# Later operand splits in two up products, S5 tables and convolution weight splits on VectorE, and a skip term folded into Toeplitz blocks

## The chip, the cores and the metric

The kernel runs on one core of one Trainium2 chip. The metric is the device time of one execution in microseconds, taken as the median of repeated runs. Five engines work side by side on a core: TensorE (PE, matrix products), VectorE (DVE), ScalarE (ACT), GpSimd (POOL) and SyncE (SP), which here issues nearly all transfers. Each executes its own instructions in the order in which they stand in its queue.

## What is computed

One layer of a diffusion backbone on 1,024 latent tokens and 256 context tokens, width 1,024, in float32:

```python
x   = half_step_ffn(x,   mods[0:3],   ffn1...)          # SwiGLU, 1024 -> 2*2816 -> 1024
ctx = half_step_ffn(ctx, mods_c[0:3], ffn1...)
# ctx passes the S5 scan once, to give the initial states h0s
p = modulate(rms_norm(x, mix_g_pre), ...) @ w_in;  bg, cg, v, u = split(p)
y_conv = bg * grid_short_conv(cg * v, conv_w)           # 512 channels
y = einsum(h_fwd, c).real + einsum(h_bwd, c).real + d_skip * u    # S5, 32 groups of 16
y = gelu(y);  y_ssm = y * sigmoid(y @ w_glu + b_glu)
x = x + mods[5] * rms_norm(concat(y_conv, y_ssm) @ w_out, mix_g_post)
x = half_step_ffn(x, mods[6:9], ffn2...)
```

`half_step_ffn` is `x + 0.5*gate*rms_norm((silu(g)*u) @ w_down)` with `g, u = split(modulate(rms_norm(x)) @ w_gu)`.

## The kernel before

**Arithmetic.** A float32 product is made of three passes: each operand is split into a high part (an ACT copy rounded to fp32r) and a low part (a DVE subtraction, operand minus high part), and PE adds high*high, high*low and low*high (`split`, L157; `hop` does it for an activation block, `wop` for a weight block, `wcols` for 128 columns of a weight). The latent up products (`g_lat`) and down products (`d_lat`) use a seven-product scheme: the tokens are two halves, the contraction is two halves, and products numbered 1 to 7 take blocks b11, b21, b12, b22 or their differences.

**Start of an up product.** `hops` (L562) goes through the stages 1, 2, 5, 3, 7, 6, 4, with four blocks (k = 0 to 3) in each. In stages 1, 2, 5 and 3 PE transposes the normalised tokens into PSUM and ACT evacuates a block with scale and shift; stages 5, 7, 6 and 4 subtract blocks in place on DVE. Each stage then splits its four blocks (`hop`: one ACT copy and one DVE subtraction of 128x512 each), one step behind. While this runs, PE does sixteen early products: for the first four column blocks f = 0 to 3 of the weight the products 1, 2, 5, 3, straight in float32 without splits. The first split products are (0,6), (1,6), (0,7), (1,7), (0,4), (1,4), then the same of f = 2, 3; the blocks of stage 2 and of stage 3 are first needed split by (4,2) and (4,3). The interleaving of `hops` steps (h), products (p, P), weight preparations (w) and norm steps is written out by hand in the strings `S1` (first up product) and `S2` (second).

**Order.** The order on each engine is fixed at build time by a scheduler that walks along a simulated timeline and takes the earliest ready instruction of the program. In the start of the first up product DVE and PE are held to program order (`G0`); in the second they are not.

**Context stage.** `g_ctx` makes the context's up product in 22 blocks f of 48 matmuls of 256 columns; a block's two weights are split one block ahead by `wcols`. Beside it runs `s5_prep`, which makes the S5 tables: four groups o of eight scan groups, each with six 128x1024 multiplications, additions or subtractions (`cmul`, in `s5_prep`, L1395), then transposes and small matmuls on PE. For o = 0 and 2 the six run on DVE, for o = 1 and 3 on POOL. At its end it builds the Toeplitz blocks of the short lags; lag zero is the tile `lag0`.

**Convolution and S5 stage.** `conv` (L1644) makes twelve products of 128 columns of `w_in` (48 matmuls each), whose weights `wcols` splits one weight ahead; the pattern `PC` puts six of the subtractions on POOL and the others on DVE. Its steps cover sixteen `s5_pair` steps: PE, then DVE (four short reductions, eight operations of 128x256 and two scans), then POOL (two multiplications of 128x512), DVE again, and PE, which waits for the result. After each four pairs `s5_out` (L1619) brings the result back through DRAM, loads `u` again (512 KB), adds the skip term `u*d` on DVE (128x1024) and applies the GELU. The string of numbers `UNITS` says how many convolution steps follow each pair.

Of the kernel before, what the change touches and what calls it, by code (L numbers as in the profile page):

```python
# [13 lines left out]
OP = mybir.AluOpType  # L14
AX = mybir.AxisListType

P = 128
# [7 lines left out]
G = 32  # L25
PAIRS = G // 2
H = 16
# [41 lines left out]
class Kernel:  # L69
# [492 lines left out]
    def hops(self, stages, blocks, hb, hr):  # L562

        t = [[], []]
        for src, m in stages:
            if src:
                x, f = src
                mm, one = blocks[x]  # L570
                if not t[x]:
                    t[x] = [self.z([P, 2, 512]) for _ in range(4)]
                pts = [mm(k + 4 * f) for k in range(4)]
                yield
            pend = None
            for k in range(4):
                if src:
                    one(k + 4 * f, t[x][k][:, f], pts[k])
                b11, b21 = (t[0][k][:, q] for q in range(2))
                b12, b22 = (t[1][k][:, q] if t[1] else None for q in range(2))  # L580
                if m == 5:
                    self.sub(b11, b12, b11)
                elif m == 7:
                    self.sub(b12, b22, b12)
                elif m == 6:
                    self.sub(b11, b22, b11)
                elif m == 4:
                    self.sub(b21, b21, b11)
                c = {1: b11, 2: b21, 3: b22, 4: b21, 5: b11, 6: b11, 7: b12}[m]
                if m in hr:  # L590
                    hr[m].append(c)
                if pend is not None:
                    hb[m].append(self.hop(pend))
                pend = c
                if k < 3:
                    yield
            hb[m].append(self.hop(pend))
            yield

    def postnorm_g(self, ys, gate, xsrcs, dsts):  # L600
# [794 lines left out]
    def s5_prep(self):  # L1395
        nc, i = self.nc, self.i
        pl = nc.gpsimd
        slot = lambda shape: self.t(self.zp, shape, "z")
        crs = [slot([P, 4, 2, 64]) for _ in range(2)]
        for k, nme in enumerate(("ssm_c_re", "ssm_c_im")):  # L1400
            for d in range(2):
                self.load(crs[k][:, :, d, :], i[nme][0, d].rearrange("(b g) h p -> (g h) b p", b=4))
        pw, br_ = slot([P, 2, 2, T8, 32]), slot([P, 2, 32, H])
        self.load(pw.rearrange("p w r t a -> p (w r t a)"), self.pwd)
        self.load(br_.rearrange("p r a h -> p (r a h)"), self.brd)
        yield
        czp = [slot([P, 32, 2, H]) for _ in range(2)]
        ct = slot([P, 2, 32, H])
        for k in range(2):
            pl.memset(czp[k], 0.0)  # L1410
        for _ in range(4):
            yield
        for k in range(2):
            pt = self.ps()
            for b in range(4):
                self.tr(pt[:, b * P : (b + 1) * P], crs[k][:, b].rearrange("p d n -> p (d n)"), P)
            self.ts(ct[:, k].rearrange("p a h -> p (a h)"), pt, 1.0 - 2 * k)
            for d in range(2):
                r = slice(64 * d, 64 * d + 64)
                nc.scalar.activation(czp[k][r, :, d, :], ct[r, k], AF.Copy)  # L1420
            yield
        kt_ = slot([P, G, 32])
        pdv = self.pd.rearrange("a p w -> p a w")
        shp = [P, 8, T8, H]

        def power(w, r, gs):
            return pw[:, w, r, :, gs].rearrange("p t a -> p a t").unsqueeze(3).to_broadcast(shp)

        for o in range(4):
            gs = slice(8 * o, 8 * o + 8)  # L1430
            xr, xi, xt = slot(shp), slot(shp), slot(shp)
            b0 = br_[:, 0, gs, :].unsqueeze(2).to_broadcast(shp)
            b1 = br_[:, 1, gs, :].unsqueeze(2).to_broadcast(shp)
            self.cmul(xr, xi, power(0, 0, gs), power(0, 1, gs), b0, b1, xt, pl if o % 2 else None)
            yield
            pk = self.ps()
            for a in range(8):
                for r, xx in ((0, xr), (1, xi)):
                    nc.tensor.matmul(
                        pk[:, 32 * a : 32 * a + 32],  # L1440
                        xx[:, a].rearrange("p t h -> p (t h)"),
                        czp[r][:, 8 * o + a].rearrange("p q h -> p (q h)"),
                        start=r == 0,
                        stop=r == 1,
                    )
            nc.vector.tensor_copy(kt_[:, gs, :], pk[:, :256].rearrange("p (a n) -> p a n", n=32))
            yield
            for r, xx in ((0, xr), (1, xi)):
                ev = slot([P, 8, P])
                for b in range(2):  # L1450
                    pt = self.ps()
                    for a in range(4):
                        self.tr(
                            pt[:, a * P : (a + 1) * P],
                            xx[:, 4 * b + a].rearrange("p t h -> p (t h)"),
                            P,
                        )
                    nc.scalar.activation(
                        ev[:, 4 * b : 4 * b + 4, :], pt.rearrange("p (a n) -> p a n", n=P), AF.Copy
                    )  # L1460
                c0 = BO + 256 * r
                self.load(
                    pdv[:, 4 * o : 4 * o + 4, c0 : c0 + 256], ev.rearrange("p (a q) n -> p a (q n)", q=2)
                )
                yield

        lag0 = slot([H, G, H])
        self.load(lag0, kt_[112:128, :, 0:H])
        self.add(lag0, lag0, kt_[0:16, :, H:])
        for t in range(T8):  # L1470
            r = slice(t * H, t * H + H)
            if t < 7:
                self.load(self.gd[:, :, 14 - t], kt_[r, :, 0:H])
            if t > 0:
                self.load(self.gd[:, :, 7 - t], kt_[r, :, H:])
        self.load(self.gd[:, :, 7], lag0)
        yield
        for t in range(T8):
            r = slice(t * H, t * H + H)
            self.load(self.td[r], self.gd[:, :, 7 - t : 15 - t].rearrange("h g l k -> h g (l k)"))  # L1480
            if t % TY == TY - 1:
                yield
        self.load(self.ctd, ct.rearrange("p r a h -> p (r a h)"))
# [135 lines left out]
    def s5_out(self, j, yps, dst=None):  # L1619
        nc = self.nc  # L1620
        ye = self.z([P, 4, 2, CL])
        for q in range(2):
            nc.scalar.activation(ye[:, :, q, :], yps[q].rearrange("p (a c) -> p a c", c=CL), AF.Copy)
        ydf = self.yd.rearrange("t h g c -> (t h) g c")
        self.load(ydf[:, 8 * j : 8 * j + 8, :], ye.rearrange("p a q c -> p (a q) c"))
        y = self.ta() if dst is None else dst
        yv = y.rearrange("p (t c) -> p t c", t=T8)
        for g in range(8):
            self.load(yv[H * g : H * g + H], self.yd[:, :, 8 * j + g, :].rearrange("t h c -> h t c"))
        u = self.ta()  # L1630
        self.load(u, self.ud[j * P : (j + 1) * P].rearrange("p t c -> p (t c)"))
        yield
        self.stt(y, u, self.ssmd(j), y, OP.mult, OP.add)
        nc.scalar.activation(u, y, AF.Square, scale=math.sqrt(0.044715))
        self.stt(u, u, 1.0, y, OP.add, OP.mult)
        nc.scalar.activation(u, u, AF.Tanh, scale=math.sqrt(2.0 / PI))
        self.stt(y, u, 1.0, y, OP.add, OP.mult)
        self.td_(u)
        if dst is None:
            self.load(self.zd[j], y)  # L1640
            self.td_(y)
        yield

    def conv(self, hi, lo, yc):  # L1644
# [5 lines left out]
        for p, c0 in enumerate(seq):  # L1650
# [5 lines left out]
            for h in range(2):  # L1656
# [3 lines left out]
                if h == 0 and p + 1 < len(seq):  # L1660
                    nxt = self.wcols(win, seq[p + 1], nc.gpsimd if PC[p % len(PC)] else None)
                if n == 0:
# [464 lines left out]


PP = PH = PU = 0
PC = (0, 1, 0, 0, 1, 0, 1, 1, 0, 1, 1, 1)  # L2130
FIVE = 4
SW = 520
QE = 0
# [70 lines left out]
```

## Time and profile before

| | us |
|---|---|
| median of 3 runs | 2041.51 |
| the three runs | 2045.14, 2041.51, 2039.92 |
| the profiled execution, its own time | 2045.32 |
| its span, first to last instruction | 2043.5 |
| PE busy in the span | 1949.4 (95%) |
| DVE busy | 1419.7 (69%) |
| ACT busy | 830.8 (41%) |
| POOL busy | 111.5 (5%) |
| mean granted TensorE clock | 0.985 of full speed |

The span and 1.8 us around it make the profiled time, which is 3.8 us above the median. PE is busy in all but 94 us of the span, so what a change can win lies in these 94 us, and in stretches where the clock granted to PE was below full speed. A row of the timeline tells when a run of equal instructions on an engine started, how long it took, how many there were (x), and in brackets how long the engine stood idle before it and what ended that.

### The profile page before, as it was taken

What the parts mean: (1) busy time and instruction counts of PE and PEld (TensorE: products, weight loads), DVE (VectorE), ACT (ScalarE), POOL (GpSimd) and SP (SyncE); (2) the same over time, 40 slices, a digit from 0 to 9 for tenths busy, and PEclk for the clock granted to TensorE, in tenths of its full rate; (3) what the DMA queues carried; (4) which work ended last, traced back from release to release, by engine and by line L of the source; (5) the groups of instructions that cost most, each with busy time, mean ns of one, the idle gap of its engine ahead of it and who ended that gap; (6) DMA issues with size and microseconds to landing.
All of it is one profiled execution on the core that took longest, in us unless ns stands there. A gap on an engine that the chain in (4) does not pass through costs nothing.

```text
span 2043.5 us, 25754 instructions
## 1 busy us (share of the span) xinstructions
PE 1949.4 (95%) x9364; PEld 1554.5 (76%) x9364; DVE 1419.7 (69%) x2548; ACT 830.8 (41%) x1463; POOL 111.5 (5%) x70
## 2 busy tenths in 40 slices
PE   7899999999899999999998899998999999999997
PEld 3477778888898978778787778764888888887775
DVE  1774459897753669797759885488855555577977
ACT  5432333434343445575432333364333333334543
POOL 0000000000420000000004430010000000000000
PEclk9999999999999999999999999998999999999999
DMA  9157642555679875566785433331632222277554
GB/s 331 31 191 255 249 141 83 144 158 162 196 222 257 284 262 176 199 234 232 215 279 165 165 113 114 103 124 56 206 110 73 93 88 78 88 269 271 185 183 162
DMA packets 328251, 354.94 MB, mean 174 GB/s; under 512 B 46976, under 2 KB 242236, under 8 KB 328124
## 3 DMA queue, kind: packets, MB, share of 16 engines
q1 hardware_dynamic: 325820, 344.91, 51.8%
q10 hardware_dynamic: 2304, 8.39, 1.0%
q8 instruction: 73, 1.20, 0.2%
q14 instruction: 54, 0.44, 0.1%
HBM read 280.61 MB, written 74.69 MB: 174 GB/s over the span
## 4 chain that ended last, share of the span: by engine, by line
PE 74%; DVE 15%; DMA 5%; issue 2%; ACT 2%; SPq 1%; POOL 1%; DVEq 0%; ACTq 0%; POOLq 0%
PE ps L51 74%; DVE z L51 6%; DVE t L51 5%; DVE w L51 3%; DMA wr<-in_ffn_w_down 1%; SPq L51 1%; DMA wr<-in_ffn_w_gu 1%; ACT t L51 1%; DMA z<-in_w_ada 1%; ACT w L51 1%; ACT z L51 1%; DMA z<-in_x 0%; POOL t L51 0%; DVE sy L51 0%; DMA wr<-t2d 0%
## 5 line engine op out<-in xcount | busy, mean ns | idle before, releaser
L51 PE MATMUL ps<-z,w 128*128 128x512 f32 (+1 forms) x5328 | 1144.4, 375 | 21.2 <-DVE w L51 6.9
L51 PEld LDWEIGHTS ps<-z,w 128*128 128x128 f32 x5328 | 931.2, 191 | 216.3 <-DVE w L51 7.9
L51 PE MATMUL ps<-w,w 128*128 128x512 f32 x1848 | 426.8, 392 | 15.4 <-DVE w L51 10.7
L51 PEld LDWEIGHTS ps<-w,w 128*128 128x128 f32 x1848 | 346.6, 188 | 93.8 <-DVE w L51 15.1
L51 ACT ACTIVATE w<-wr 128x512 fp32r<-128x512 f32 (+1 forms) x270 | 206.8, 767 | 360.3 <-PE ps L51 302.8
L51 DVE TENSOR_TENSOR w<-wr,w 128x512 fp32r<-128x512 f32 (+1 forms) x264 | 234.3, 889 | 117.5 <-ACT w L51 114.8
L51 ACT ACTIVATE w<-t 128x512 fp32r<-128x512 f32 x292 | 177.5, 626 | 183.0 <-DVE t L51 88.1
L51 DVE TENSOR_TENSOR w<-t,w 128x512 fp32r<-128x512 f32 x292 | 197.4, 687 | 75.1 <-ACT w L51 74.8
L51 DVE TENSOR_TENSOR t<-t,ps 128x512 f32<-128x512 f32 x150 | 102.5, 685 | 109.0 <-PE ps L51 108.3
L51 PE MATMUL ps<-z,t 128*128 128x512 f32 x512 | 147.1, 448 | 9.9 <-DVE t L51 8.8
L51 PEld LDWEIGHTS ps<-z,t 128*128 128x128 f32 x512 | 96.8, 190 | 58.3 <-issue 37.5
L51 ACT ACTIVATE t<-ps 128x512 f32<-128x512 f32 (+2 forms) x143 | 77.4, 542 | 147.8 <-PE ps L51 146.3
L51 ACT ACTIVATE w<-z 128x512 fp32r<-128x512 f32 x110 | 69.5, 632 | 144.7 <-PE ps L51 142.6
L51 DVE TENSOR_TENSOR z<-z,z 128x512 fp32r<-128x512 f32 (+3 forms) x139 | 114.3, 856 | 16.7 <-ACT z L51 11.7
L51 DVE TENSOR_TENSOR t<-wr 128x512 f32<-128x512 f32 x124 | 83.6, 686 | 20.3 <-DMA wr<-in_ffn_w_down 13.4
L51 ACT ACTIVATE t<-z 128x1024 bf16<-128x1024 f32 (+3 forms) x132 | 75.5, 605 | 48.4 <-DVE z L51 31.6
L51 DVE TENSOR_TENSOR w<-z,w 128x512 fp32r<-128x512 f32 x110 | 75.6, 687 | 24.2 <-ACT w L51 24.0
L51 ACT ACTIVATE t<-t 128x512 f32<-128x512 f32 (+1 forms) x83 | 51.8, 624 | 74.0 <-DVE t L51 73.3
L51 DVE TENSOR_TENSOR z<-t,ps 128x512 f32<-128x512 f32 (+1 forms) x52 | 29.8, 573 | 64.4 <-PE ps L51 64.4
L51 ACT ACTIVATE z<-z 128x512 fp32r<-128x512 f32 (+2 forms) x76 | 48.0, 678 | 56.0 <-DVE z L51 42.2
L51 PE MATMUL ps<-w,t 128*128 128x512 f32 x264 | 64.4, 401 | 1.9 <-DVE w L51 1.3
L51 ACT ACTIVATE z<-ps 128x512 f32<-128x512 f32 x74 | 41.6, 595 | 56.6 <-PE ps L51 56.5
(120 smaller groups left out, 1333.7 us busy)
## 6 DMA issues: line engine op xcount, KB each, us to landing
wr<-in_ffn_w_gu SPq DMA_DIRECT2D x136, 512.0 KB, 4.3
wr<-in_ffn_w_down SPq DMA_DIRECT2D x198, 256.0 KB, 3.7
tb<-in_w_ada SPq DMA_DIRECT2D x56, 512.0 KB, 6.0
sd<-z SPq DMA_DIRECT2D x44, 512.0 KB, 3.1
z<-sd SPq DMA_DIRECT2D x88, 256.0 KB, 5.2
wr<-in_ffn_w_down SPq DMA_DIRECT2D x22, 512.0 KB, 4.5
wr<-in_w_in SPq DMA_DIRECT2D x20, 512.0 KB, 4.7
z<-in_w_ada SPq DMA_DIRECT2D x16, 512.0 KB, 6.4
```

Source lines behind the costliest of these rows:

```text
L51: r = f(*a, **kw)
```

## The change

Four edits. (1) In `hops` the splits of stage 2 are made in stage 4, each just ahead of the subtraction that overwrites its block, and those of stage 3 after all other stages; this holds for both up products. (2) In `s5_prep` all four groups of tables run on DVE. (3) The skip term leaves `s5_out`, with its load of `u`; instead `d` is loaded once as a 16x32 table, spread over a diagonal and added to `lag0`, so that the Toeplitz product carries it. (4) `PC` becomes `(0,)`: all twelve convolution weights are split on DVE.

```diff
@@ hops
                 elif m == 4:
+                    hb[2].append(self.hop(b21))
                     self.sub(b21, b21, b11)
...
-                if pend is not None:
+                if pend is not None and m not in (2, 3):
                     hb[m].append(self.hop(pend))
                 pend = c
                 if k < 3:
                     yield
-            hb[m].append(self.hop(pend))
+            if m not in (2, 3):
+                hb[m].append(self.hop(pend))
+            yield
+        for k in range(4):
+            hb[3].append(self.hop(t[1][k][:, 1]))
             yield
@@ s5_prep
+        dg = self.t(self.cp, [H, G], "dg")
+        self.load(dg, i["ssm_d"][0].rearrange("(g h) -> h g", h=H))
...
-            self.cmul(xr, xi, power(0, 0, gs), power(0, 1, gs), b0, b1, xt, pl if o % 2 else None)
+            self.cmul(xr, xi, power(0, 0, gs), power(0, 1, gs), b0, b1, xt)
...
         self.add(lag0, lag0, kt_[0:16, :, H:])
+        skip = slot([H, G, H])
+        nc.vector.tensor_tensor(
+            skip, dg[:, :].unsqueeze(2).to_broadcast([H, G, H]),
+            self.ident[:H, :H].unsqueeze(1).to_broadcast([H, G, H]), OP.mult,
+        )
+        self.add(lag0, lag0, skip)
@@ s5_out
-        self.load(u, self.ud[j * P : (j + 1) * P].rearrange("p t c -> p (t c)"))
-        yield
-        self.stt(y, u, self.ssmd(j), y, OP.mult, OP.add)
+        yield
@@
-PC = (0, 1, 0, 0, 1, 0, 1, 1, 0, 1, 1, 1)
+PC = (0,)
```

## Rows read from the trace of the kernel before

**Rows 1.** Busy time by stretch: length, PE, PEld, DVE, ACT, POOL, granted clock, DMA

```profile
92.80:110.00 17.20, 8.30 (x26) 5.34 (x26) 15.46 (x26) 7.97 (x14) 0.00 (x0) 0.79 0.41 121
...
520.00:600.00 80.00, 74.28 (x575) 73.54 (x574) 56.45 (x47) 30.07 (x43) 32.24 (x12) 0.91 0.68 208
...
1070.00:1222.00 152.00, 134.47 (x702) 114.29 (x701) 136.67 (x320) 48.09 (x110) 61.96 (x41) 0.97 0.46 151
...
1400.00:1425.00 25.00, 16.17 (x36) 6.85 (x34) 19.82 (x34) 5.09 (x9) 0.00 (x0) 0.80 0.22 66
```

**Rows 2.** Timeline of PE, start of the first up product

```profile
65.32 27.63 PE L51 MATMUL ps<-z,t 128*128 128x512 f32 x64
...
109.80 40.69 PE L51 MATMUL ps<-z,w 128*128 128x512 f32 x168 [3.00 <-DVE tb L51]
```

**Rows 3.** Timeline of DVE, the same start

```profile
71.00 1.89 DVE L51 TENSOR_TENSOR z<-z,z 128x512 fp32r<-128x512 f32 x3
...
86.13 0.69 DVE L51 TENSOR_TENSOR t<-t,ps 128x512 f32<-128x512 f32 x1 [2.34 <-PE ps L51]
...
109.07 0.68 DVE L51 TENSOR_TENSOR tb<-tb,ps 128x512 f32<-128x512 f32 x1
```

**Rows 4.** Timeline of PE, start of the second up product

```profile
1387.05 13.90 PE L51 MATMUL ps<-z,t 128*128 128x512 f32 x32
1409.78 15.73 PE L51 MATMUL ps<-z,t 128*128 128x512 f32 x32 [8.83 <-DVE t L51]
```

**Rows 5.** Timeline of DVE, the same start

```profile
1366.20 3.69 DVE L51 TENSOR_TENSOR z<-z,z 128x512 fp32r<-128x512 f32 x6
...
1392.11 4.90 DVE L51 TENSOR_TENSOR z<-z,z 128x512 fp32r<-128x512 f32 x8
...
1402.35 0.68 DVE L51 TENSOR_TENSOR t<-tb,ps 128x512 f32<-128x512 f32 x1
...
1408.95 2.49 DVE L51 TENSOR_TENSOR t<-wr,t 128x512 f32<-128x512 f32 x4
```

**Rows 6.** Timeline of PE, context stage

```profile
544.56 5.06 PE L51 MATMUL ps<-z,w 128*128 128x256 f32 x22 [5.72 <-DVE w L51]
...
550.78 6.54 PE L51 MATMUL ps<-z,w 128*128 128x256 f32 x53
```

**Rows 7.** Timeline of DVE, context stage

```profile
533.16 8.06 DVE L51 TENSOR_TENSOR z<-z,z 128x1024 f32<-128x1024 f32 x3
541.15 3.35 DVE L51 TENSOR_TENSOR w<-wr,w 128x1024 fp32r<-128x1024 f32 x1
...
581.03 3.49 DVE L51 TENSOR_TENSOR z<-z,z 128x1024 f32<-128x1024 f32 x3
```

**Rows 8.** Timeline of POOL, context stage

```profile
525.80 17.62 POOL L51 TENSOR_TENSOR z<-z,z 128x1024 f32<-128x1024 f32 x6 [20.55 <-DMA z<-brd]
```

**Rows 9.** Timeline of DVE, convolution and S5 stage

```profile
1079.54 3.63 DVE L51 TENSOR_TENSOR t<-t,t 128x256 f32<-128x256 f32 x4
...
1095.88 1.54 DVE L51 TENSOR_TENSOR t<-t,t 128x256 f32<-128x256 f32 x4
...
1154.61 1.28 DVE L51 SCALAR_TENSOR_TENSOR z<-z,cols,z 128x1024 f32<-128x1024 f32 x1
...
1199.26 3.37 DVE L51 SCALAR_TENSOR_TENSOR z<-z,cols,z 128x960 f32<-128x960 f32 x1
```

**Rows 10.** Timeline of POOL, convolution and S5 stage

```profile
1080.45 2.44 POOL L51 TENSOR_TENSOR w<-wr,w 128x1024 fp32r<-128x1024 f32 x1 [1.02 <-ACT w L51]
...
1199.11 2.50 POOL L51 TENSOR_TENSOR w<-wr,w 128x1024 fp32r<-128x1024 f32 x1 [4.12 <-ACT w L51]
```

**Rows 11.** Waits of 1070 to 1222 us: total, times, longest

```profile
PE ps L51 <- DVE t L51: 15.8, 7, 5.9
```

**Rows 12.** Groups by form, 1035 to 1245 us: busy, mean ns, idle before

```profile
L51 DVE SCALAR_TENSOR_TENSOR z<-z,cols,z 128x1024 f32<-128x1024 f32 x4 | 5.6, 1398 | 4.3 <-DMA z<-yd 4.3
...
L51 POOL TENSOR_TENSOR w<-wr,w 128x1024 fp32r<-128x1024 f32 x6 | 15.6, 2605 | 66.0 <-ACT w L51 66.0
```

**Rows 13.** Transfers: queue, count, KB each, us to landing

```profile
z<-ud SPq DMA_DIRECT2D x4, 512.0 KB, 6.2
...
t<-in_ssm_log_dt SPq DMA_DIRECT2D x1, 0.2 KB, 2.9
```

## The prediction

> **What bounds the kernel now.** I read the busy time by stretch first, to find the stretches in which PE is not full: only there can edits on other engines pay. Four of them are touched by the change [rows 1]: the start of the first up product (8.9 us of 17.2 without PE work, clock 0.79), the context stage (5.7 of 80 us, clock 0.91), the convolution and S5 stage (17.5 of 152 us, clock 0.97), and the start of the second up product (8.8 of 25 us, clock 0.80). Then, at the end of each hole, the timeline of PE names what ended the wait, and the timelines of DVE and POOL show what that engine did until then. Each time it is DVE: an add for which PE waited 3.00 us [rows 2], a weight split after 5.72 us [rows 6], a weight operand after 8.83 us [rows 4], and in the S5 stage 15.8 of the 17.5 us [rows 11]. So the question at every edit is whether DVE gets to that instruction earlier or later.
>
> **Tables on DVE (context stage).** The six POOL operations of o = 1 run from 525.80 for 17.62 us [rows 8]. Beside them three DVE operations took 8.06 us and a weight split 3.35 us; without POOL three of the same take 3.49 us [rows 7], 1.16 us each. DVE loses 8.06 - 3.49 = 4.6 us on the three and 3.35 - 1.16 = 2.2 us on the split, 6.8 us ahead of the split for which PE stood 5.72 us. The Trainium skill (SBUF — State Buffer, Who interferes with whom) says that a VectorE operation with two SBUF inputs and a GpSimd operation that reads SBUF exclude each other for a whole instruction; rows 7 agree, as each DVE operation took the length of a POOL one. Without POOL that split ends 6.8 us earlier, so the 5.72 us go. After the hole PE ran 22 matmuls in 5.06 us, 0.230 each, against 53 in 6.54 us, 0.123 each [rows 6], that is at the lower of its two clocks (1.2 GHz in place of 2.4): 22 x 0.107 = 2.4 us more. Against this DVE gets twelve operations, 12 x 1.16 = 13.9 us, in a stretch where it has 80 - 56.5 = 23.5 us free [rows 1] plus what the contention held. I take -8.1 us; bounds -10 (dips elsewhere in the stage, too) and -3 (the new operations stand ahead of some weight split). The skip table's two small operations and one more transfer of 2 KB (the nearest row, also made of single elements, lands in 2.9 us [rows 13]) come long before `lag0` is used; two DVE operations are at most 2 x 0.69 us by the 128x512 rows [rows 3] and lie beside PE work: 0.
>
> **Convolution splits and skip term (S5 stage).** The stage is DVE's: 136.67 of 152 us busy [rows 1]. A POOL split takes 2.6 us, six of them 15.6 [rows 12]. Five fall into the stage, and beside each a DVE group is stretched: the first 3.63 us in place of 1.54, 2.1 us more, the last 3.37 us for an instruction of 960 columns where one of 1,024 took 1.28 us, again 2.1 [rows 9 and 10]. Five times 2.1 is 10.5 us of DVE time that goes. The splits come back as 5 x 1.16 = 5.8 us. Three of the four skip operations lie in the stage, 1.4 us each [rows 12]: 4.2 us that go. The four reloads of u with 512 KB [rows 13] go from SP's queue; the S5 chain of the next pairs gains nothing from this that a row shows, 0. Net for DVE: -10.5 + 5.8 - 4.2 = -8.9 us. PE waited 15.8 us for DVE here, so there is room for all of it: -9 us. Bounds: -4 if half of it falls where PE is not waiting, -16 if all DVE waits go. By the Trainium skill (Perfetto Trace Analysis, Optimizing Scalar/DVE Operations) work may be moved from a saturated VectorE to GpSimd, which speaks against edit 4, though the page adds that the shared port may spoil it. By the first half alone the stage would gain nothing; that is the first rival.
>
> **Late splits, first up product.** Here DVE is in program order. The stage-3 splits stood around 71 us [rows 3], the stage-2 splits before that. DVE then waits 2.34 us at 86.13 for PE, which runs its early products without a gap from 65.32 to 92.8 [rows 2 and 3]. Eight splits fewer before 86 us only lengthen that wait; nothing is won. After it DVE is full to 109.07 (15.46 of 17.2 us [rows 1]), where the add stands that lets PE go on. The stage-2 splits now come in stage 4 and the stage-3 splits behind it, all in that full stretch: 8 x 0.60 us (1.89 us for three, with overlap [rows 3]) = 4.8 us. How many stand ahead of the add is the scheduler's choice: none gives 0, all give +4.8. As their ACT copies wait for nothing, they are ready early and will be taken; I take five, +3 us.
>
> **Late splits, second up product.** DVE works off 27 splits and subtractions, counted in the same timeline from 1385 on, before the add at 1402.35; PE, idle since 1400.95 (1387.05 + 13.90), gets its operand at 1408.95 and goes on at 1409.78 [rows 4 and 5]. The four stage-3 splits are among the 27 (4 x 0.61, eight took 4.90 [rows 5]) = 2.4 us that go from ahead of the wait. The stage-2 splits lay near 1366 to 1370 [rows 5], where PE had float32 products to do: 0. Without program order, though, the scheduler may fill the place with later splits: then 0. If it moves the adds up, the whole 8.83 us and the slow 15.73 against 13.90 us [rows 4] can go, -10.6. I take -2.
>
> **The sum.** -8.1 - 9 + 3 - 2 = -16 us. Against the profiled execution (2043.5 span and 1.8 around it, 2045.3) that is 2029; the profiled run lies 3.8 us above the median 2041.5, so for the median 2025.5.
>
> **The rivals.** (a) DVE stays the bound of the S5 stage: the returned splits stand in the pair chain, and the stretched DVE operations were ones PE didn't wait for. For it: DVE is 90% busy there. Against: nothing but DVE lies behind 15.8 us of waits, and the sum for DVE is negative. Then -8.1 + 0 + 3 + 0 = -5: 2036.5. (b) All DVE waits go: -8.1 - 15.8 - 10.6 + 3 = -31.5: 2010. For it: the waits are short and few (seven in the S5 stage); against: shortening a queue by 9 us seldom removes 15.8. (c) Slower: in the S5 stage the convolution weights now queue on DVE behind the pairs. A pair takes DVE 136.67 / 16 = 8.5 us; PE lives on one weight for 48 matmuls x 0.242 (40.69 us for 168 [rows 2]) = 11.6 us. A split that stands two pairs back, 17 us, makes PE wait 5.4 us. Five times that is +27 in place of -9: with -8.1, +3 and -2 it is +20, 2061. It decides from more than one pair of delay on. Against: the six splits already on DVE cause none of the seven waits above. (d) The change does not do what it says: the order chosen at build time puts other work into the places that come free, and the holes stay. Then no change, 2041.5.
>
> **How the numbers follow.** Forecast 0.50, with its own range 2018 to 2033; (a) 0.20; (b) 0.15; (c) 0.10; (d) 0.05. About 0.3% (6 us) is what a measurement can tell from no change. Faster by more: nearly all of the forecast, all of (b) and nearly half of (a), 0.72. Within it: the rest of (a), (d), 0.18. Slower: (c), 0.10. The range 2009 to 2039 takes in the forecast, (a) and (b) and leaves out (c), (d) and a little of each end.
>
> **What would show it.** Right: no wait of PE for a weight split between 520 and 600 us, and DVE operations of 128x1024 at 1.2 us throughout; in the S5 stage no DVE row of 128x256 stretched by 2 us except beside POOL's own multiplications, and PE's waits for DVE near 7 us in place of 15.8; four 128x1024 skip rows and four loads of u gone; in the first start DVE waiting longer for PE near 83 us and the hole after 92.8 longer by some 3 us; in the second the hole near 6.5 us. Wrong: a PE wait for a weight split in the S5 stage (c), the same 15 us of waits there (a), or a hole at either start that changes by over 5 us.

## The result, and the profile after

| | before | after |
|---|---|---|
| median, us | 2041.65 (4 runs) | 2025.20 (4 runs) |
| runs from, to | 2039.92 to 2045.14 | 2021.52 to 2027.74 |
| profiled execution, us | 2045.32 | 2025.27 |
| its span, us | 2043.5 | 2023.5 |
| mean granted clock | 0.985 | 0.988 |

The ratio is 0.9907, with a 95% interval of 0.9894 to 0.9921: faster. The medians lie 16.4 us apart; the prediction said 16 (2025.5). The ratio itself stands for 19 us (16 to 22 by its interval). The two profiled executions lie 20 us apart, as the one of before was 3.7 us above its median and the one of after at its own. The total hides terms that were wrong in size. To see this I took, in both traces, the start of the same PE rows at the borders of the stages, and subtracted the lengths of the stretches between them:

| stretch, border rows of PE | after minus before, us | predicted |
|---|---|---|
| up to the context stage, first start in it | -0.2 | +3 |
| context stage | -8.0 | -8.1 |
| context's down product to the S5 stage | +2.0 | |
| S5 stage (first `ps<-tb,z` group to last `ps<-t,z`) | -7.1 | -9 |
| on to the second up product | -0.3 | |
| its start, hole and float32 products | -8.9 | -2 |
| rest of it and last down product | +2.5 | |

Single stretches of one execution are not exact: in the other kernels run here, whose code from the first split products of the second up product on is that of before or of after, the last stretch differs from before by -2.2 to +3.8 us. What was edited is larger than that in three places, and each has its row.

Busy time by stretch of the kernel after (columns as in [rows 1]); the third stretch is the S5 stage, the fourth the second start:

```profile
92.80:110.00 17.20, 11.03 (x29) 7.96 (x30) 15.26 (x26) 9.16 (x16) 0.00 (x0) 0.70 0.38 108
520.00:600.00 80.00, 80.00 (x649) 79.45 (x649) 54.85 (x58) 33.12 (x47) 0.00 (x0) 0.96 0.75 227
1063.80:1208.60 144.80, 134.38 (x703) 114.15 (x701) 131.35 (x323) 48.12 (x110) 48.23 (x36) 0.98 0.46 153
1380.00:1402.00 22.00, 20.50 (x48) 8.68 (x47) 22.00 (x38) 8.39 (x15) 0.00 (x0) 1.00 0.20 55
```

In the context stage PE is busy for all 80 us, where it was idle for 5.7; at the second start it is idle for 1.5 of 22, where it was idle for 8.8 of 25 [rows 1]. At the first start DVE is nearly full as before; PE is idle for some 6 us of 17.2 in place of 8.9, at a lower clock, 0.70 in place of 0.79.

**Context stage.** Groups by form of DVE from 520 to 640 us (busy, mean ns | idle before):

```profile
L51 DVE TENSOR_TENSOR w<-wr,w 128x1024 fp32r<-128x1024 f32 x32 | 39.1, 1222 | 20.4 <-ACT w L51 17.2 <-DMA wr<-in_ffn_w_gu 1.6 <-DMA z<-in_ssm_c_re 1.3
L51 DVE TENSOR_TENSOR z<-z,z 128x1024 f32<-128x1024 f32 x24 | 28.6, 1218 | 0.0
```

All 24 table operations and all 32 weight splits take 1.22 us; none is stretched to the 2.7 to 3.35 us of [rows 7]. Neither PE's wait of 5.72 us nor the slow 22 matmuls behind it [rows 6] have a counterpart.

**S5 stage.** PE's waits from 1063 to 1210 us (total, times, longest), and DVE's additions and subtractions of the scan pairs by form, from 1060 to 1225 us (four in each of the sixteen pairs; both inputs are `t` tiles in SBUF, the on-chip memory of the tiles, whereas the four multiplications of a pair, `t<-ps,z`, read one input from PSUM):

```profile
PE ps L51 <- DVE t L51: 7.0, 6, 3.5
...
PE ps L51 <- DMA z<-pd: 3.2, 3, 1.5
```

```profile
L51 DVE TENSOR_TENSOR t<-t,t 128x256 f32<-128x256 f32 x64 | 28.1, 467 | 5.3 <-POOL t L51 4.6
```

PE waits 7.0 us for DVE in place of 15.8 [rows 11]. The same 64 additions and subtractions took 35.3 us before, 583 ns each (its row stands with the experiments on POOL).

**Second start.** PE, then DVE:

```profile
1373.47 13.90 PE L51 MATMUL ps<-z,t 128*128 128x512 f32 x32
1388.88 14.14 PE L51 MATMUL ps<-z,t 128*128 128x512 f32 x32 [1.50 <-DVE t L51]
1402.46 67.76 PE L51 MATMUL ps<-z,w 128*128 128x512 f32 x288
```

```profile
1371.43 0.69 DVE L51 TENSOR_TENSOR z<-z,z 128x512 f32<-128x512 f32 x1 [0.49 <-ACT z L51]
...
1378.42 6.70 DVE L51 TENSOR_TENSOR z<-z,z 128x512 fp32r<-128x512 f32 x11
1385.05 0.68 DVE L51 TENSOR_TENSOR t<-tb,ps 128x512 f32<-128x512 f32 x1
...
1388.05 0.68 DVE L51 TENSOR_TENSOR t<-wr,t 128x512 f32<-128x512 f32 x1
```

The hole shrank from 8.83 to 1.50 us, and the 32 products behind it run at full clock, 14.14 us in place of 15.73 [rows 4]. DVE's operand comes 16.6 us after its first subtraction (1388.05 less 1371.43).

**First start.** PE, then DVE:

```profile
98.79 2.93 PE L51 MATMUL ps<-z,w 128*128 128x512 f32 x6 [1.98 <-DVE z L51]
102.39 13.88 PE L51 MATMUL ps<-z,w 128*128 128x512 f32 x48 [0.68 <-DVE z L51]
116.83 0.96 PE L51 MATMUL ps<-z,w 128*128 128x512 f32 x3 [0.56 <-DVE z L51]
118.63 6.55 PE L51 MATMUL ps<-z,w 128*128 128x512 f32 x27 [0.84 <-DVE z L51]
```

```profile
72.02 0.69 DVE L51 TENSOR_TENSOR t<-tb,ps 128x512 f32<-128x512 f32 x1 [1.91 <-PE ps L51]
...
85.75 0.69 DVE L51 TENSOR_TENSOR t<-t,ps 128x512 f32<-128x512 f32 x1 [2.75 <-PE ps L51]
...
107.08 0.68 DVE L51 TENSOR_TENSOR tb<-tb,ps 128x512 f32<-128x512 f32 x1
...
119.70 2.49 DVE L51 TENSOR_TENSOR z<-z,z 128x512 fp32r<-128x512 f32 x4
```

The early splits are gone from around 71 us, and DVE waits 4.7 us for PE from there to 86 us, where it waited 2.3. The add that held PE [rows 2 and 3] now stands two microseconds earlier, at 107.08, and four splits in one run come behind it, at 119.70. PE's wait of 3.00 us went, and small waits for split blocks came.

### The profile page after: what moved, and what is told of

Read it like the earlier page. It is cut to its first block, busy times and chain, and to the rows that moved or that the text cites. A ratio compares the mean times of both kernels' runs of the same rounds, so it can differ in the third digit from the quotient of the medians.

```text
span 2023.5 us, 25732 instructions
## 1 busy us (share of the span) xinstructions
PE 1949.8 (96%) x9364; PEld 1554.1 (77%) x9364; DVE 1413.8 (70%) x2564; ACT 830.3 (41%) x1463; POOL 63.1 (3%) x52
## 4 chain that ended last, share of the span: by engine, by line
PE 75%; DVE 12%; DMA 6%; ACT 2%; issue 2%; SPq 1%; POOL 0%; DVEq 0%; ACTq 0%; POOLq 0%
PE ps L51 75%; DVE z L51 5%; DVE t L51 3%; DVE w L51 3%; DMA wr<-in_ffn_w_down 2%; SPq L51 1%; DMA wr<-in_ffn_w_gu 1%; ACT w L51 1%; ACT t L51 1%; DMA z<-in_w_ada 1%; ACT z L51 1%; DMA z<-sd 1%; DMA z<-pd 1%; DMA z<-in_x 0%; POOL t L51 0%
## 5 line engine op out<-in xcount | busy, mean ns | idle before, releaser
L51 DVE TENSOR_TENSOR z<-z,z 128x512 fp32r<-128x512 f32 (+3 forms) x152 | 124.8, 853 | 12.8 <-ACT z L51 6.6
```

Of the source, the lines that this page charges most:

```text
L51: r = f(*a, **kw)
```

## The experiments

Twelve kernels, each timed beside the kernel before. Parts are given as ratio to before with its interval, and in us as that ratio times 2041.65.

### Each edit alone

The four edits, each alone in the kernel before. Edit 1 (`hops` as in the diff shown above):

> Only edit 1, the late splits in both up products. Theory: in the changed kernel's trace the start of the second up product lost 8.9 us against before (the hole 8.83 to 1.50 us, and the float32 products behind it at the full clock) and the first start 0.1; alone the edit should then give -9 us, some 2033 against 2041.7. Rival (the forecast's sizes): +3 in the first and -2 in the second, +1 us, no measurable change.

Measured 2042.26, ratio 0.9998 (0.9988 to 1.0007): no gain, so the time is the rival's. Yet PE's timeline shows the second start as in the kernel after:

```profile
1390.46 13.90 PE L51 MATMUL ps<-z,t 128*128 128x512 f32 x32
1405.87 14.14 PE L51 MATMUL ps<-z,t 128*128 128x512 f32 x32 [1.51 <-DVE t L51]
```

Something else takes back 9 us. This stayed open until the last runs of this section.

Edit 2 alone (tables on DVE):

```diff
-            self.cmul(xr, xi, power(0, 0, gs), power(0, 1, gs), b0, b1, xt, pl if o % 2 else None)
+            self.cmul(xr, xi, power(0, 0, gs), power(0, 1, gs), b0, b1, xt)
```

> Only edit 2, all S5 tables on VectorE. Theory: POOL's products kept VectorE waiting in the context stage; the stage gives -8 us (the 5.72 us wait of PE and the 2.4 us at the lower clock behind it go), VectorE's 128x1024 operations there take 1.22 us throughout, some 2033.5. Rival: VectorE only takes over 12 x 1.16 = 13.9 us and the weight splits queue behind it; then 0 to +8 us and new waits of PE for weight splits between 520 and 600 us.

Measured 2035.62, 0.9968 (0.9957 to 0.9978), -6.5 us; the context stage of the profiled execution is 8.7 us shorter.

Edit 4 alone (convolution splits on DVE):

```diff
-PC = (0, 1, 0, 0, 1, 0, 1, 1, 0, 1, 1, 1)
+PC = (0,)
```

> Only edit 4, all convolution weights split on VectorE. Theory: five POOL splits in the stage hold VectorE 2.1 us each and cost it 1.16 each when it does them itself: -4.7 us of VectorE time, -3 to -5 us of the stage, some 2037.5. Rival: VectorE is saturated there and the splits return on its chain: +2 to +6 us.

Measured 2036.42, 0.9971 (0.9961 to 0.9980), -5.9 us; the S5 stage is 6.1 us shorter.

Edit 3 alone (skip term in `lag0`, the four skip operations and the loads of `u` gone):

> Only edit 3, the skip term in the Toeplitz blocks. Theory: three operations of 1.4 us go from VectorE in the S5 stage, -4.2 us of VectorE time, -2 to -4 us of the stage, some 2038.5. Rival: they lay where PE was not waiting, 0.

Measured 2043.70, 1.0003 (0.9992 to 1.0015): nothing, and the S5 stage is 0.4 us shorter. 4.2 us of DVE work went from an engine for which PE waits 15.8 us, and the stage got shorter by a tenth of that: the rival was right.

### What POOL does to DVE

Is it POOL's reading of SBUF that stretches DVE's operations, or POOL at work at all? Two kernels put idle work on POOL behind POOL's two multiplications of every second pair of the kernel after. DVE's instructions are those of the kernel after, in nearly the same order; PE's come in a somewhat other order, so the durations on DVE say more here than the length of the stage. The first reads: two multiplications of 128x512.

```diff
         self.mul(q2, w, ei, pl)
+        if a % 2:
+            for _ in range(2):
+                with self.tc.issue_after(pl.prev):
+                    self.mul(co[:, :512].rearrange("p (a c) -> p a c", a=4), self.ident.unsqueeze(1).to_broadcast([P, 4, P]),
+                             self.ident.unsqueeze(1).to_broadcast([P, 4, P]), pl)
```

> The changed kernel with dummy work on POOL: behind POOL's two multiplications of every second S5 pair (eight of sixteen) two more multiplications of 128x512 that read SBUF and write into a tile nobody reads any more, 2.34 us each time, as long as a convolution split was. VectorE has the same instructions in the same order. Theory (two-input VectorE operations and SBUF-reading POOL operations exclude each other): VectorE operations of 128x256 beside them are stretched by up to 2 us, 8 x 2.1 = 17 us more VectorE time in the stage and +6 to +14 us in all, against the changed kernel's 2025. Rival (the moved work paid because POOL itself was late, or by a mere reordering): no change, 2025.

The second only writes: five memsets of 128x512.

```diff
         self.mul(q2, w, ei, pl)
+        if a % 2:
+            for _ in range(5):
+                with self.tc.issue_after(pl.prev):
+                    pl.memset(co[:, :512], 0.0)
```

> The same as the run with the reading dummies, but POOL fills the dead tile (five memsets of 128x512, 2.3 us in all) and reads nothing. Theory of the read port: no stretched VectorE operations, 2025 as the changed kernel. Rival (any POOL activity holds VectorE): the same loss as with the reading dummies, +6 to +14 us.

Measured: reading 2036.39, 0.9970 (0.9959 to 0.9981); writing 2023.25, 0.9913 (0.9899 to 0.9927). Groups by form from 1060 to 1225 us, reading, then writing:

```profile
L51 POOL TENSOR_TENSOR t<-ident 128x512 f32<-128x512 f32 x16 | 17.6, 1097 | 0.5
...
L51 DVE TENSOR_TENSOR t<-t,t 128x256 f32<-128x256 f32 x64 | 37.5, 612 | 6.5 <-POOL t L51 5.7
```

```profile
L51 POOL MEMSET t<- 128x512 f32 x40 | 21.0, 526 | 1.7
...
L51 DVE TENSOR_TENSOR t<-t,t 128x256 f32<-128x256 f32 x64 | 27.0, 449 | 6.4 <-POOL t L51 5.7
```

17.6 us of reading work stretches the additions and subtractions from 467 to 612 ns, and the S5 stage from 144.7 us in the kernel after to 154.6; 21.0 us of writing work leaves them at 449 ns and the stage at 143.5. So it is POOL's reads that stretch them. DVE's own multiplications of the pairs, of the same 128x256, have one input in PSUM, and POOL's reads leave them alone. POOL, then DVE, in the kernel with the reading work:

```profile
1092.68 2.34 POOL L51 TENSOR_TENSOR t<-t,z 128x512 f32<-128x512 f32 x2 [4.04 <-issue]
1094.97 2.23 POOL L51 TENSOR_TENSOR t<-ident 128x512 f32<-128x512 f32 x2
```

```profile
1093.74 1.41 DVE L51 TENSOR_TENSOR t<-ps,z 128x256 f32<-128x256 f32 x4 [0.49 <-ACT t L51]
1095.07 3.20 DVE L51 TENSOR_TENSOR t<-t,t 128x256 f32<-128x256 f32 x4
```

With POOL at work from 1092.68 to 1097.20, the four with an input in PSUM take 1.41 us and the four with both inputs in SBUF 3.20, where the like took 1.54 before [rows 9]. All 64 of the first kind take 22.7 us in the kernel before, in the one after and in both of these. The Trainium skill (SBUF — State Buffer, Who interferes with whom) says that a VectorE instruction with two SBUF inputs contends with a GpSimd instruction that reads SBUF and not with one that only writes it; both runs and these rows agree.

### More on POOL, and less

Does the hold add up with each split? The kernel before with all twelve convolution splits on POOL:

```diff
-PC = (0, 1, 0, 0, 1, 0, 1, 1, 0, 1, 1, 1)
+PC = (1,)
```

> The kernel before with the subtractions of all twelve convolution weights on GpSimd in place of six. Theory (each split on GpSimd holds VectorE for 2.1 us or more, against 1.2 us that it takes on VectorE): the mirror image of moving six back, which gave -6.1 us in the stage; five or six more on GpSimd cost +5 to +7, 2047 to 2049. Rival (VectorE is the bound of the stage and is relieved by 6 x 1.2 us): 2034 to 2037.

Measured 2044.27, 1.0006 (0.9994 to 1.0018): in neither range. Groups by form of the kernel before, then of this one, from 1060 to 1225 us:

```profile
L51 POOL TENSOR_TENSOR w<-wr,w 128x1024 fp32r<-128x1024 f32 x5 | 13.2, 2646 | 7.7 <-ACT w L51 7.7
...
L51 DVE TENSOR_TENSOR t<-t,t 128x256 f32<-128x256 f32 x64 | 35.3, 583 | 5.5 <-POOL t L51 4.7
...
L51 DVE SCALAR_TENSOR_TENSOR z<-z,cols,z 128x896 f32<-128x896 f32 x4 | 6.3, 1578 | 0.1
...
L51 DVE TENSOR_TENSOR w<-wr,w 128x1024 fp32r<-128x1024 f32 x3 | 4.6, 1523 | 0.1
```

```profile
L51 POOL TENSOR_TENSOR w<-wr,w 128x1024 fp32r<-128x1024 f32 x8 | 20.3, 2538 | 20.0 <-ACT w L51 20.0
...
L51 DVE TENSOR_TENSOR t<-t,t 128x256 f32<-128x256 f32 x64 | 38.6, 634 | 5.5 <-POOL t L51 4.7
...
L51 DVE SCALAR_TENSOR_TENSOR z<-z,cols,z 128x896 f32<-128x896 f32 x4 | 7.5, 1874 | 1.3 <-ACT z L51 1.2
```

Of the splits that moved only three fall into the stage. They take 4.6 us from DVE, stretch its additions and subtractions by 38.6 - 35.3 = 3.3 us and the operations of 896 columns by 7.5 - 6.3 = 1.2 us, 4.5 us together: gain and price cancel. PE waits 15.9 us for DVE, as before. The price of 2.1 us for each split, which I carried over from [rows 9 and 10], is that of the five that were there, not of any split: these three cost 1.5 us each.

And the last step in the other direction: the kernel after, with the two multiplications of each pair on DVE too.

```diff
-        self.mul(q1, w, er, pl)
-        self.mul(q2, w, ei, pl)
+        self.mul(q1, w, er)
+        self.mul(q2, w, ei)
```

> The kernel after with the two multiplications of each scan pair also on VectorE, so that in the S5 stage GpSimd keeps four instructions. VectorE gets 32 x 0.68 = 22 us more in the stage and is no longer held by them (64 operations of 128x256 at 0.467 could go to 0.38, 6 us, and 5 us of waits for GpSimd end). Theory (moving pays only where an instruction holds VectorE for longer than VectorE needs for it itself; these multiplications of 1.37 us mostly run while VectorE waits for them or reads PSUM): VectorE's work rises by some 11 to 16 us net, the stage grows by 5 to 12, 2031 to 2037. Rival (any GpSimd instruction that reads SBUF costs more than it saves, so the last ones should go too, and each pair's chain gets shorter by 1.4 us): 2018 to 2023.

Measured 2027.46, 0.9925 (0.9910 to 0.9941): between the rival's range and the theory's. In its profiled execution the S5 stage is 6.2 us longer than in the kernel after, the way from there to the second up product 2.1 shorter. PE waits 12.5 us for DVE in place of 7.0. Its interval overlaps that of the kernel after (0.9894 to 0.9921), so by the times it is no gain, and perhaps a loss; in the stage the theory's +5 to +12 us came. Groups by form, 1060 to 1225 us:

```profile
L51 DVE TENSOR_TENSOR t<-t,t 128x256 f32<-128x256 f32 x64 | 27.1, 445 | 1.0
...
L51 DVE TENSOR_TENSOR t<-t,z 128x512 f32<-128x512 f32 x32 | 20.7, 688 | 0.6
```

32 operations add 20.7 us to DVE. They free 1 us of its additions and subtractions and some 5 us of waits for POOL, and other operations there shorten too; in sum DVE's busy time in the stage still rises from 131.3 to 144.2 us.

### The late splits, one product at a time

In the kernel after, the late splits in the second product only (a flag to `hops`, off for the first):

```diff
-    def hops(self, stages, blocks, hb, hr):
+    def hops(self, stages, blocks, hb, hr, late=True):
...
-                if pend is not None and m not in (2, 3):
+                if pend is not None and not (late and m in (2, 3)):
```

> The changed kernel with the late splits in the second up product alone; the first has them in place as before. Theory: the first start did not change (0.1 us), so the same as the changed kernel, 2025 within 2 us. Rival (forecast): 3 us faster than the changed kernel, 2022.

Measured 2020.98, 0.9901 (0.9884 to 0.9917); by the ratio 1 us less than the kernel after. And in the first product only:

> The changed kernel with the late splits in the first up product alone. Theory: the second start's hole of 8.8 us and the lower clock behind it come back, +9 us against the changed kernel, 2034. Rival (forecast): +2 us, 2027.

Measured 2029.96, 0.9943 (0.9925 to 0.9961); the hole of 8.83 us is back:

```profile
1399.86 16.44 PE L51 MATMUL ps<-z,t 128*128 128x512 f32 x32 [8.83 <-DVE t L51]
```

Inside the kernel after, then, undoing the second product's late splits costs 0.9943 - 0.9907, some 7 us; undoing the first one's gains 0.0006, 1 us, within the intervals. That doesn't fit edit 1 alone, which gained nothing. The same two cuts in the kernel before, first the second product only:

> The kernel before with late splits in the second up product only; the first one keeps its order. Late splits alone, in both products, had given 2042.3, no gain in the median, although the hole of 8.83 us at the second start was gone in its trace. Theory (the gain at the second start is real, and what took it back came with the changed order of the first start): about 2034, 8 us under the kernel before, hole gone. Rival (without the other three edits something later in the run gives the gain back, whatever the first start does): 2042, hole gone, and the time from the first split products of the second up product to the end longer than before by several us. Second rival (both sit below what one set of runs can tell): between the two, 2037 to 2040.

Measured 2031.78, 0.9948 (0.9932 to 0.9965): -10.6 us, nearest to the theory. And the first product only:

> The kernel before with late splits in the first up product only. With both late splits the kernel before gained nothing (2042.3), with those of the second alone it gained 10.6 us by the ratio (2031.8), so the first should account for the difference. Its own stretch, from the first early product to the 168 or more products behind the hole, grew by only 0.1 us; but the order of transfers on SP's queue that is fixed at build time comes out otherwise in the context stage and the S5 stage when the first start is changed, while nothing there was edited. Theory (the changed order further down costs what the second start gains): 2050 to 2054, with the S5 stage 2 us longer and the context stage no shorter. Rival (the two edits don't add; alone the first costs only the 1 us or so of its own stretch): 2042 to 2045.

Measured 2049.69, 1.0037 (1.0025 to 1.0049): +7.6 us, a hair under the 2050 that the theory asked for and outside the rival's 2042 to 2045. So edit 1 alone is -10.6 + 7.6 = -3.0, which agrees with the measured 0 within the intervals: the first product's late splits ate what the second one's gave. The loss is not at the first start, whose stretch did not grow. Part of it is in the S5 stage, in which nothing was edited and which is 2.5 us longer. Busy time of the stage, before and here (columns as in [rows 1]):

```profile
1070.02:1221.83 151.81, 134.28 (x701) 114.12 (x699) 136.50 (x320) 48.09 (x110) 61.96 (x41) 0.97 0.46 151
```

```profile
1069.49:1223.81 154.32, 137.37 (x701) 116.59 (x700) 137.13 (x320) 48.05 (x110) 61.84 (x41) 0.94 0.46 155
```

PE is idle for no longer than before, 16.9 us against 17.5; the same 701 matmuls take it 3.1 us more, at a lower clock. What differs is the order on SP's queue, fixed at build time. SP's queue of the kernel before, then of this one (start, duration, transfer):

```profile
1108.48 0.32 SPq L51 DMA_DIRECT2D yd<-z  x1
...
1117.99 1.45 SPq L51 DMA_DIRECT2D z<-pd  x2
...
1134.61 0.32 SPq L51 DMA_DIRECT2D zd<-z  x1
1134.98 0.42 SPq L51 DMA_DIRECT2D z<-ud  x1
1135.49 4.60 SPq L51 DMA_DIRECT2D z<-pd  x2
```

```profile
1118.14 0.43 SPq L51 DMA_DIRECT2D z<-td  x1
1129.09 0.32 SPq L51 DMA_DIRECT2D zd<-z  x1
1129.46 0.42 SPq L51 DMA_DIRECT2D z<-ud  x1
1129.97 1.28 SPq L51 DMA_DIRECT2D z<-pd  x2
```

The store `zd<-z` needs the result of a 128x1024 operation of DVE:

```profile
1127.85 1.21 DVE L51 SCALAR_TENSOR_TENSOR z<-z,z 128x1024 f32<-128x1024 f32 x1
```

In the kernel before two loads `z<-pd` were ahead of that store and left at 1117.99. Here they stand behind it: SP waits from 1118.6 to 1129.1 for DVE (whose operation ends at 1129.06), the loads leave at 1129.97, and PE, which had no wait for a transfer at this place, waits for them:

```profile
1135.55 1.05 PE L51 MATMUL ps<-tb,z 128*128 128x160 f32 x6 [1.99 <-DMA z<-pd]
```

In place of one hole of 5.88 us for DVE, PE has three waits here, of 1.99, 3.39 and 0.61 us. They come to as much, but in the 10 us from 1139.5 on the granted clock is 0.63, where it was 0.82 in those from 1140.0 on. Edit 1 alone has the same order in this stage, the same wait (2.34 us), the clock of 0.94 and a stage 2.3 us longer. That the new order is what lowers the clock is argued from these two kernels; no run changes the one without the other. The kernel after with and without the late splits of the first product has one and the same order on SP in the S5 stage, in a stage that edits 3 and 4 have changed; there the first product's late splits cost 1 us in place of 7.6. Of these 7.6, 2.5 are seen in the rows; the other 5 I could not place in single profiled executions, whose stretches vary by as much, and their cause stays open.

It fits that the parts don't add up. The four edits alone come to -0.4 - 6.5 + 0.6 - 5.9 = -12.2 us, together by the ratio to -19.0. The 7 us between are about what the first product's late splits cost in the kernel before and not in the one after.

## Why the prediction was right, and where it was not

**Tables on DVE: -8.1, came as -8.0** in the profiled executions (-6.5 by the times of edit 2 alone). The step held as written: three operations and a split that no longer last as long as POOL's, a hole of PE that goes with its slow matmuls. The twelve operations that DVE got came in free stretches: between 500 and 690 us PE waits for a weight split three times, none over 0.9 us, 2.1 us in all, where before it was 6.9.

**S5 stage: -9, came as -7.1.** The mechanism held: POOL's reads hold DVE, the splits back on DVE shorten it, PE's waits for DVE are 7.0, where "near 7" had been said, and (c), a PE wait for a weight split on DVE, has no row in the stage. What was mis-sized is the skip term: -4.2 us in the sum, and 0 alone (1.0003, the stage 0.4 us shorter); its operations are four long ones in `s5_out`, whose time was not what held up the stage. Without it the step reads -10.5 + 5.8 = -4.7, and edit 4 alone gave -5.9. PE's waits for DVE shrank by 8.8 us and the stage by 7.1, because waits for transfers `z<-pd`, which the prediction did not price, grew from 1.5 to 3.2 us.

**First start: +3, came as 0.** "As their ACT copies wait for nothing, they are ready early and will be taken" failed: the four stage-3 splits, which `hops` makes last, stand behind the add, at 119.70. With the stage-2 splits in it, stage 4 is stretched out too: one of its four subtractions stands ahead of the add (104.06), where all four did (103.05 to 108.47), and the add itself stands at 107.08 instead of 109.07. The longer wait of DVE ahead of it was there as said (1.91 + 2.75 us). The bound of +4.8 was no bound, though: alone in the kernel before, this edit costs 7.6 us, and what rows show of it, 2.5 us of slower matmuls, lies 1,000 us later. The missing step, as far as the runs show it, was the shared scheduler: a different first start gives a different order of transfers on SP further down. That this order is the whole cost is not shown. In the kernel after, where edits 3 and 4 had changed that place, the cost is 1 us; this is luck of the combination, not a term that I had worked out.

**Second start: -2, came as -8.9** (-10.6 by the times, alone; some -7 inside the kernel after). The step that failed is the choice within the bounds 0 to -10.6. I counted only the four stage-3 splits as leaving the 27 in front of the add. In front of the first add stand 21 splits and subtractions now: four splits fewer, as counted, but two subtractions fewer as well, and 13.6 us pass in place of 17.2. And the operand comes after two adds, not four, 3.0 us behind the start of the first add in place of 6.6, because the scheduler moved it up. From first subtraction to operand 16.6 us pass, where 23.8 did. The 10.6 had been listed with its condition, "if it moves the adds up", and that is what it did, but for the 1.5 us of the hole that stayed. The clock followed: 14.14 us at full clock for 32 products that took 15.73 behind the long hole [rows 4]. That the times of this edit alone give 10.6 too is chance: in its trace the second start gains 8.9, and the context stage, in which nothing was edited, is 3.6 us shorter. Which of the two kinds of late split moved the operand no run tells.

**The sum.** +3 too dear, -9 two too good, -2 seven too small, and 4.5 us lost in stretches that the prediction had not named (2.0 behind the context stage, 2.5 at the end, the latter within what single executions differ by). The 7 and 3 us in its favour nearly met the 2 and 4.5 against it, and the rest of the 20 us is the distance of the execution before from its median. The total is closer than its terms deserve: that is luck.

**Rivals.** (a) fell: PE's waits in the S5 stage halved. (b) was nearly right for the second start alone, where all but 1.5 us of the wait went. (c) fell. (d) fell, but its thought, that the order chosen at build time decides, was right twice, in both directions.

The fastest kernel here is the one after with the early splits of the first product kept (2020.98), 4.2 us below the median of after; their intervals overlap, so it is not shown to be better.

## What to carry to other kernels

Work on POOL that reads SBUF is not free help for DVE: price it by the rows of DVE beside it, and only those of operations with both inputs in SBUF. Where a build-time scheduler fixes all queues, an edit's price is not bounded by its own stretch: compare the order on the transfer queue over the whole program, and try each edit alone and taken out of the whole, since the two differed here by 6 us (7.6 against 1). When a queue is what holds PE, count all that stands in front of the operand on that engine, what stands between the first add and the operand too, and ask what order the scheduler will choose when some of it goes.

## What was not expected of the hardware

40 memsets on POOL, 21.0 us of them, left DVE's additions and subtractions and the length of the stage as they were, while 16 multiplications on POOL of 17.6 us in all cost the stage 10 us. DVE's operations of the same size with one input in PSUM took 1.41 us for four beside these, and 22.7 us for all 64 in every one of the four kernels compared. And a split on POOL had no fixed price for DVE: five in the stage stretched a group by 2.1 us each, three more cost 4.5 us together.
